# A Mamba/mLSTM/MoE block and a Hyena/RWKV block in one kernel: which engine makes the experts' low parts, and how the Hyena filters' last layer is multiplied

## The chip, the cores and the metric

The kernel runs on one core of a Trainium2 chip. The metric is the device time of one execution in microseconds (us): the median over the runs. Engines are named as in the profile: PE (TensorE matmul), PEld (its weight load), DVE (VectorE), ACT (ScalarE), POOL (GpSimd), SP (SyncE, which here only issues DMAs).

## The reference

One sequence of 1,024 tokens with 1,024 features passes two blocks. The first block mixes by an SSD and an mLSTM half and then by a mixture of 32 experts, two of them for each token. The second block mixes by Hyena (long convolutions, whose filters come from a small network) and RWKV halves, and ends with a feed-forward layer. Two pieces matter here:

```python
def hier_moe(h, wg, bg, we, be, w_gate, w_up, w_down):
    ...
    hg = lax.ragged_dot(xs, w_gate.astype(xs.dtype), sizes)
    hu = lax.ragged_dot(xs, w_up.astype(xs.dtype), sizes)
    ys = lax.ragged_dot(jax.nn.silu(hg) * hu, w_down.astype(xs.dtype), sizes)
    ...

def hyena_filters(L, fw1, fb1, fw2, fb2, fw3, fb3, fw4, sin_freq):
    ...
    h = jnp.sin(sf[0] * (feats @ fw1.astype(f32) + fb1.astype(f32)))
    h = jnp.sin(sf[1] * (h @ fw2.astype(f32) + fb2.astype(f32)))
    h = jnp.sin(sf[2] * (h @ fw3.astype(f32) + fb3.astype(f32)))
    h = (h @ fw4.astype(f32)).reshape(L, HY_ORDER, 2, HY_WIDTH)
    ...
    window = jnp.exp(-t * deltas[None, :])
    return h * window[:, None, None, :]
```

`fw4` has 64 rows and 2 x 2 x 512 columns. Everything is float32, and the filters depend on no token.

## The kernel before, in words

**How a float32 product is made.** `split` (lines 108 to 116) cuts a float32 tile into a high part, a copy of type F32R made by ScalarE (line 112), and a low part, the tile less the high part, an F32R tile made by a subtraction on VectorE or on an engine that the caller names (line 113). A product then is three F32R matmuls: high by high, high by low and low by high (`mm3`, line 125, and the experts' own loops at lines 989 and 1010). Matmuls on plain F32 operands are used in few places; the filter network is one.

**Experts (lines 954 to 1014).** Each of the 32 experts handles up to 128 gathered tokens (a loop behind them takes what is over). GpSimd clears the tile `X` (line 960) and gathers the tokens (961); PE transposes them, and `split` makes XTh and XTl. `wload` (972) fetches a weight matrix in pieces of 512 KB from a ring of raw buffers (`eraw`, and for the first experts also `ahead`), and splits it into `ewh` and `ewl`, four buffers each. There are four such pieces (q = 0 to 3) for each of the three matrices, 12 for each expert. The low part of piece q = 1 is made on GpSimd and the other three on VectorE: in all 96 on GpSimd and 288 on VectorE, which also makes the low parts of the tokens and of the hidden activations (XTl, Hl) and the gating (995, 996). ScalarE writes the expert's output `Y` (1012), and GpSimd adds it to memory by a scattered DMA (1013). SP issues the loads of the raw buffers.

**Filters (lines 1152 to 1250).** From expert 8 on, `moe` advances a generator once for each expert, so that the filters of the second block are computed between the experts' steps. It loads the small network and the DFT matrix, runs three sine layers of 64 outputs (matmul 1183, VectorE 1184 to 1191, Sin on ScalarE 1193), reorders the last one into `h3` by two VectorE copies (1198), and then, for each of two orders and two halves of the channels, loads 64 x 2 x 256 of `fw4` (1204) and for eight blocks of 128 positions makes two F32 products of 256 columns with 64 rows in the contraction (1215), multiplies each by the window on VectorE (`hfb`, 1217), and forms their sum and their difference on GpSimd (`hsum` 1220, `hd` 1223). These are split (`hsh` on ScalarE, `hsl` on VectorE, 115 and 116) and go through a DFT of F32R matmuls; GpSimd combines its outputs (`HR`, `HS`, line 1252).

**What sets the order.** The program is written as generators that advance in turn, and the Tile framework then lists each engine's instructions by a simulated timeline of the whole program. An edit can therefore move instructions on any engine, also far behind the place that it touches. One such place is the end of the RWKV recurrence: `rwkv_norm` (1957 to 1995) reads the recurrence's output `ytok`, adds its two directions, normalises (`ya`, ScalarE, line 1983) and transposes it (1987), while the last chunk of the recurrence still runs (`cup` on PE, line 1771; its copy `cUV` on ScalarE, 1775; `cyp` on PE, 1804; `cY`, 1811; `ytok`, 1813), and the gated projection of the Hyena output (`rwkv_out`, 2014: `yr<-hz_d`, `mwr`, then matmuls `mps<-yrh,mwh` through line 125) waits to start on the same queues.

Of the kernel before, what the change touches and what calls it, by code (L numbers as in the profile page):

```python
# [20 lines left out]
F32 = mybir.dt.float32  # L21
F32R = mybir.dt.float32r
# [3 lines left out]
ALU = mybir.AluOpType  # L26
# [4 lines left out]
P = 128  # L31
# [10 lines left out]
def f32(ap):  # L42
    return ap.bitcast(F32)
# [6 lines left out]
class Kern:  # L50
# [904 lines left out]
    def expert(self, ep, psm, pst, pg, gi, gate, wg, wu, wd, next_raw):  # L955
# [198 lines left out]
    def hyena_filters(self, psm, p, w):  # L1154
# [3 lines left out]
        self.hs_d = self.dp.tile([2, 2, P, 4, 512], F32, name="hs_d")  # L1158
        feats = w.tile([33, L], F32, name="feats", tag="hA", bufs=1)
        nc.sync.dma_start(feats, T["c_feats"])  # L1160
        fw = [p.tile([n, 64], F32, name=f"fw{i}") for i, n in enumerate((33, 64, 64))]
        for i in range(3):
            nc.sync.dma_start(fw[i], I[f"hy_filt_w{i + 1}_2"][0])
        fb = p.tile([64, 3], F32, name="fb")
        sf = p.tile([64, 3], F32, name="sf")
        for i in range(3):
            nc.sync.dma_start(fb[:, i:i + 1], I[f"hy_filt_b{i + 1}_2"][0].rearrange("(p o) -> p o", o=1))
        nc.sync.dma_start(sf, I["hy_sin_freq_2"][0].rearrange("l p -> p l"), allow_slow_non_contiguous=True)
# [6 lines left out]
        h = feats  # L1175
        MAGIC = 12582912.0
        for i in range(3):
            a = w.tile([64, L], F32, name="fa", tag="HR", bufs=1)
            n = w.tile([64, L], F32, name="fn", tag="HS", bufs=1)
            for half in range(2):  # L1180
                sl = slice(half * 512, half * 512 + 512)
                ps = psm.tile([64, 512], F32, name="fps", tag="s")
                nc.tensor.matmul(ps, fw[i], h[:, sl], start=True, stop=True)
                nc.vector.tensor_scalar(a[:, sl], ps, fb[:, i:i + 1], sf[:, i:i + 1], op0=ALU.add, op1=ALU.mult)
# [7 lines left out]
            h = w.tile([64, L], F32, name="fh", tag="hA", bufs=1)  # L1192
            nc.scalar.activation(h, a, AF.Sin)
            yield
        h3 = p.tile([64, 8, P], F32, name="h3")

        for mb in range(2):
            nc.vector.tensor_copy(h3[:, mb * 4:mb * 4 + 4],
                                  h[:, mb * 512:mb * 512 + 512].rearrange("p (m r) -> p r m", r=4))
        for o in range(2):  # L1200
            for half in range(2):
                ch = slice(half * 256, half * 256 + 256)
                fw4 = w.tile([64, 2, 256], F32, name="fw4")
                nc.sync.dma_start(fw4, w4[:, o, :, ch])
                sk = w.tile([1, 256], F32, name="hsk", bufs=1)
                nc.sync.dma_start(sk, I["hy_skip_2"][:, o, ch])
                sp = [p.tile([P, 8, 256], F32R, name=f"hs{x}") for x in "hl"]
                hd = p.tile([P, 8, 256], F32, name="hd")
                for b in range(8):
                    win = w.tile([P, 256], F32, name="win")  # L1210
                    nc.scalar.activation(win, delt[:, ch], AF.Exp, scale=tcol[:, b:b + 1])
                    hf = []
                    for d in range(2):
                        ps = psm.tile([P, 256], F32, name="fps2", tag="s")
                        nc.tensor.matmul(ps, h3[:, b], fw4[:, d], start=True, stop=True)
                        t = w.tile([P, 256], F32, name=f"hfb{d}")
                        nc.vector.tensor_tensor(t, ps, win, op=ALU.mult)
                        hf.append(t)
                    s_ = w.tile([P, 256], F32, name="hsum", bufs=1)
                    nc.gpsimd.tensor_tensor(s_, hf[0], hf[1], op=ALU.add)  # L1220
                    if b == 0:
                        nc.vector.tensor_tensor(s_[0:1], s_[0:1], sk, op=ALU.add)
                    nc.gpsimd.tensor_tensor(hd[:, b], hf[0], hf[1], op=ALU.subtract)
                    self.split(sp[0][:, b], sp[1][:, b], s_, 1.0 / 1024.0)
                    if b % 2:
                        yield
                for kb in range(2):
                    HR = w.tile([P, 4, 256], F32, name="HR", bufs=1)
                    ab, ch_ = self.dft(psm, w, Fh, Fl, sp, kb, "C")
                    _, d = self.dft(psm, w, Fh, Fl, sp, kb, "S", (1,))  # L1230
                    self.bf(HR[:, 0], ab[:, 0], ab[:, 1], ALU.add)
                    self.bf(HR[:, 1], ab[:, 0], ab[:, 1], ALU.subtract)
                    self.bf(HR[:, 2], ch_[:, 0], d[:, 0], ALU.add)
                    self.bf(HR[:, 3], ch_[:, 0], d[:, 0], ALU.subtract)
                    nc.sync.dma_start(self.hr_d[o, kb][:, :, ch], HR)
                    yield
                sp = [p.tile([P, 8, 256], F32R, name=f"hs{x}") for x in "hl"]
                for b in range(8):
                    self.split(sp[0][:, b], sp[1][:, b], hd[:, b], 1.0 / 1024.0)
                for kb in range(2):  # L1240
                    HS = w.tile([P, 4, 256], F32, name="HS", bufs=1)
                    ef, gd = self.dft(psm, w, Fh, Fl, sp, kb, "S")
                    _, h_ = self.dft(psm, w, Fh, Fl, sp, kb, "C", (1,))
                    self.bf(HS[:, 0], ef[:, 0], ef[:, 1], ALU.add)
                    self.bf(HS[:, 1], ef[:, 1], ef[:, 0], ALU.subtract)
                    self.bf(HS[:, 2], h_[:, 0], gd[:, 0], ALU.subtract)
                    self.bf(HS[:, 3], h_[:, 0], gd[:, 0], ALU.add)
                    nc.sync.dma_start(self.hs_d[o, kb][:, :, ch], HS)
                    yield
# [1052 lines left out]
```

## Time and profile before

| | |
|---|---|
| median of three runs | 3980.1 us (3979.16 to 3992.83) |
| the profiled execution's own time | 3969.92 us |
| its span in the trace | 3967.6 us |
| mean granted clock of PE | 0.937 |
| busy share PE, PEld, DVE, ACT, POOL | 89%, 72%, 72%, 38%, 39% |
| low parts `ewl<-eraw` on VectorE | 243, mean 1658 ns |
| low parts `ewl<-eraw` on GpSimd | 81, mean 2658 ns |

The span runs from the first to the last recorded instruction; the profiled execution took 2.3 us more than that, and 10.2 us less than the median. Busy shares are averages over stages with different limits, so the rows below are read stage by stage: the experts without filter work (1214 to 1352 us after the span's start), the experts with filter work (1352 to 1905), and the end of the RWKV recurrence (around 3017 to 3046).

### The profile page before, as it was taken

Reading aid. Unit: us, or ns where it says so; the run is one execution under the profiler, and the core shown is the slowest. Engines: PE = TensorE matmul, PEld = TensorE weight load, DVE = VectorE, ACT = ScalarE, POOL = GpSimd, SP = SyncE. Lnnn points to the kernel's source line nnn. Section 1 sums busy time; section 2 is a strip of 40 time slices with the busy share of each in tenths; the row PEclk is TensorE's granted clock in tenths of the full one; section 3 lists DMA queues with packets and bytes.
Section 4 is the critical chain, followed back from the end, with each engine's and each line's share of the span. In section 5 each row is a group of like instructions: output and inputs, shape, how many; then the busy total and the mean of one; then the engine's idle time right before and its main releaser. Section 6 shows DMA issues by size and latency. Waiting matters only on the chain. (4 is left out here: it accounts for less than half of the span.)

```text
span 3967.6 us, 52346 instructions
## 1 busy us (share of the span) xinstructions
PE 3544.1 (89%) x19799; PEld 2845.8 (72%) x19799; DVE 2861.4 (72%) x3992; ACT 1503.4 (38%) x2166; POOL 1540.5 (39%) x882
## 2 busy tenths in 40 slices
PE   6999897988978889999879999999776999999897
PEld 6888776666766667777656767887564777888775
DVE  7767858776457889998755887411995577777798
ACT  4332333433226766666633333222123213222331
POOL 4444434553015568777601222000771212223353
PEclk8999997899979999999989999999887999999998
DMA  4222224444568778888854777666556722222521
GB/s 102 96 85 107 97 74 148 137 151 145 182 208 285 233 247 287 294 268 274 280 153 132 213 207 194 185 192 220 161 170 195 258 103 69 85 75 95 177 94 69
DMA packets 540591, 669.34 MB, mean 169 GB/s; under 512 B 151819, under 2 KB 352015, under 8 KB 539824
## 3 DMA queue, kind: packets, MB, share of 16 engines
q1 hardware_dynamic: 429136, 535.38, 42.3%
q10 hardware_dynamic: 101984, 113.79, 8.4%
q0 software_dynamic: 9216, 16.81, 1.9%
q8 instruction: 157, 2.57, 0.3%
q14 instruction: 98, 0.80, 0.1%
HBM read 500.72 MB, written 181.83 MB: 172 GB/s over the span
## 5 line engine op out<-in xcount | busy, mean ns | idle before, releaser
L113 DVE TENSOR_TENSOR ewl<-eraw,ewh 128x1024 fp32r<-128x1024 f32 x243 | 398.8, 1658 | 40.6 <-ACT ewh L112 40.3
L112 ACT CAST ewh<-eraw 128x1024 fp32r<-128x1024 f32 x324 | 334.5, 1049 | 114.1 <-PE pgu L989 51.5
L125 PE MATMUL g<-x2h,wl 128*128 128x512 f32 x688 | 279.2, 406 | 0.0
L125 PE MATMUL g<-x2h,wh 128*128 128x512 f32 x688 | 278.9, 406 | 0.1
L125 PE MATMUL g<-x2l,wh 128*128 128x512 f32 x688 | 277.7, 404 | 0.0
L125 PE MATMUL g<-h,sw 128*128 128x512 f32 (+1 forms) x752 | 243.9, 401 | 20.5 <-ACT sw L112 9.6
L113 POOL TENSOR_TENSOR ewl<-eraw,ewh 128x1024 fp32r<-128x1024 f32 x81 | 215.3, 2658 | 111.1 <-ACT ewh L112 103.0
L163 POOL TENSOR_TENSOR sraw<-sraw 128x1024 f32<-128x1024 f32 x24 | 74.0, 3083 | 431.8 <-DVE sw L113 419.9
L125 PE MATMUL g<-xl,sw 128*128 128x512 f32 x616 | 241.5, 392 | 0.0
L989 PE MATMUL pgu<-ewl,XTh 128*128 128x512 f32 x512 | 210.5, 411 | 28.6 <-POOL ewl L113 18.0
L112 ACT CAST sw<-sraw 128x1024 fp32r<-128x1024 f32 x144 | 148.8, 1048 | 207.0 <-PE g L125 156.2
L125 PE MATMUL g<-z 128*128 128x512 f32 x820 | 201.7, 395 | 22.7 <-DVE z L113 19.7
L125 PE MATMUL g<-sw,h 128*128 128x256 f32 x960 | 184.6, 294 | 22.9 <-DVE sw L113 17.8
L989 PE MATMUL pgu<-ewh,XTh 128*128 128x512 f32 x512 | 204.2, 401 | 0.7 <-ACT XTh L112 0.7
L989 PE MATMUL pgu<-ewh,XTl 128*128 128x512 f32 x512 | 202.8, 396 | 0.0
L125 PEld LDWEIGHTS g<-z 128*128 128x128 f32 x820 | 155.1, 190 | 60.0 <-DVE z L113 23.0
L125 PEld LDWEIGHTS g<-h,sw 128*128 128x128 f32 (+1 forms) x752 | 143.2, 191 | 57.1 <-ACT sw L112 10.5
L113 DVE TENSOR_TENSOR wl<-raw,wh 128x1024 fp32r<-128x1024 f32 x43 | 52.6, 1223 | 173.1 <-ACT wh L112 167.7
L125 PEld LDWEIGHTS g<-sw,h 128*128 128x128 f32 x960 | 158.0, 202 | 23.9 <-DVE sw L113 18.6
L113 POOL TENSOR_TENSOR sw<-sraw,sw 128x1024 fp32r<-128x1024 f32 x39 | 102.5, 2628 | 179.9 <-ACT sw L112 179.9
L499 DVE SCALAR_TENSOR_TENSOR u<-sC,cw,u 128x1023 f32<-128x1023 f32 (+2 forms) x84 | 164.6, 1975 | 1.7 <-ACT u L497 1.4
L193 DVE TENSOR_TENSOR sC<-sU,g 128x512 f32<-128x512 f32 x140 | 95.2, 682 | 89.1 <-PE g L125 86.5
(684 smaller groups left out, 10113.7 us busy)
## 6 DMA issues: line engine op xcount, KB each, us to landing
eraw<-in_exp_w_down SPq DMA_DIRECT2D x112, 512.0 KB, 5.7
eraw<-in_exp_w_up SPq DMA_DIRECT2D x108, 512.0 KB, 4.7
eraw<-in_exp_w_gate SPq DMA_DIRECT2D x104, 512.0 KB, 5.6
sraw<-in_w_in SPq DMA_DIRECT2D x12, 2048.0 KB, 7.8
raw<-in_w_in ACTq DMA_DIRECT2D x43, 512.0 KB, 4.5
SC<-SC SPq DMA_DIRECT2D x32, 512.0 KB, 3.6
cSA<-X SPq DMA_DIRECT2D x32, 512.0 KB, 4.6
cSC<-SC SPq DMA_DIRECT2D x32, 512.0 KB, 7.6
```

Source lines behind the costliest of these rows:

```text
L112: nc.scalar.copy(h, raw)
L113: (eng or nc.vector).tensor_tensor(l, raw, f32(h), op=ALU.subtract)
L125: nc.tensor.matmul(ps, a, b, start=i == 0, stop=i == n - 1)
L163: Q(A11, A11, A21, op=ALU.subtract)
L193: V(c, x, ps, op=ALU.add)
L499: nc.vector.scalar_tensor_tensor(u[:, j:], x[:, :L - j], cw[:, ct, 3 - j:4 - j], u[:, j:], op0=ALU.mult, op1=ALU.add)
L989: nc.tensor.matmul(ps, a[:, q * 2 + k], b[:, k], start=q == 0 and k == 0 and i == 0, stop=q == 3 and k == 1 and i == 2)
```

## The change

The diff, cut to its core:

```diff
         def wload(w, q, down=False):
             shape = [P, D] if down else [P, 2, 512]
-            eng = nc.gpsimd if q == 1 else nc.vector
             raw = next_raw(self.piece(w, q, down))
...
-            self.split(h, l, raw, eng=eng)
+            self.split(h, l, raw)
             return h, l
...
-        fw = [p.tile([n, 64], F32, name=f"fw{i}") for i, n in enumerate((33, 64, 64))]
+        fw = [p.tile([n, m], F32, name=f"fw{i}") for i, (n, m) in enumerate(((33, 64), (64, 64), (64, P)))]
+        fb = p.tile([P, 3], F32, name="fb")
+        sf = p.tile([P, 3], F32, name="sf")
...
+            for o in range(0, fw[i].shape[1], 64):
+                nc.sync.dma_start(fw[i][:, o:o + 64], I[f"hy_filt_w{i + 1}_2"][0])
+        for o in (0, 64):
...
-        h3 = p.tile([64, 8, P], F32, name="h3")
+        h3 = p.tile([P, 8, P], F32R, name="h3")
         for mb in range(2):
-            nc.vector.tensor_copy(h3[:, mb * 4:mb * 4 + 4],
-                                  h[:, mb * 512:mb * 512 + 512].rearrange("p (m r) -> p r m", r=4))
+            x = h[:, mb * 512:mb * 512 + 512].rearrange("p (m r) -> p r m", r=4)
+            b = h3[:, mb * 4:mb * 4 + 4]
+            nc.scalar.copy(b, x)
+            nc.vector.tensor_tensor(b[64:], x[64:], f32(b)[64:], op=ALU.subtract)
...
-                fw4 = w.tile([64, 2, 256], F32, name="fw4")
-                nc.sync.dma_start(fw4, w4[:, o, :, ch])
+                fw4 = w.tile([P, 2, 256], F32, name="fw4")
+                for q in (0, 64):
+                    nc.sync.dma_start(fw4[q:q + 64], w4[:, o, :, ch])
+                fw4s = [w.tile([P, 2, 256], F32R, name=f"fw4{x}", bufs=1) for x in "hl"]
+                self.split(*fw4s, fw4)
...
-                    hf = []
-                    for d in range(2):
-                        ps = psm.tile([P, 256], F32, name="fps2", tag="s")
-                        nc.tensor.matmul(ps, h3[:, b], fw4[:, d], start=True, stop=True)
-                        t = w.tile([P, 256], F32, name=f"hfb{d}")
-                        nc.vector.tensor_tensor(t, ps, win, op=ALU.mult)
-                        hf.append(t)
+                    ps = psm.tile([P, 2, 256], F32, name="fps2", tag="s")
+                    for i in range(2):
+                        nc.tensor.matmul(ps, h3[:, b], fw4s[i], start=i == 0, stop=i == 1)
+                    hf = w.tile([P, 2, 256], F32, name="hfb")
+                    nc.vector.tensor_tensor(hf, ps, win[:, None, :].to_broadcast([P, 2, 256]), op=ALU.mult)
...
-                    nc.gpsimd.tensor_tensor(s_, hf[0], hf[1], op=ALU.add)
+                    nc.gpsimd.tensor_tensor(s_, hf[:, 0], hf[:, 1], op=ALU.add)
```

The first part gives all 384 low parts of the expert weights to VectorE. The second part computes the third sine layer twice, on partitions 0 to 63 and again on 64 to 127 (its weights, biases and frequencies are loaded twice). Then `h3` holds the high part of the layer's output in its first 64 partitions and the low part in the other 64, `fw4` stands in both halves and is split into a high and a low tile, and one contraction over 128 partitions with each of the two gives the whole product: for each block two F32R matmuls of 512 columns instead of two F32 ones of 256, and one multiplication of 128 x 512 instead of two of 128 x 256. The sums and differences on GpSimd stay.

The order of the instructions moves with it. On VectorE, among the first experts (`ewl_...` comes from raw buffers with running numbers), the low parts that GpSimd had fall into place between the others:

```order
 L113 TENSOR_TENSOR ewl<-eraw_9613,ewh 128x1024
+L113 TENSOR_TENSOR ewl<-eraw_9625,ewh 128x1024
 L113 TENSOR_TENSOR ewl<-eraw_9637,ewh 128x1024
 L113 TENSOR_TENSOR ewl<-eraw_9649,ewh 128x1024
 L113 TENSOR_TENSOR XTl<-pt,XTh 128x512
 L113 TENSOR_TENSOR ewl<-eraw_9675,ewh 128x1024
+L113 TENSOR_TENSOR ewl<-eraw_9687,ewh 128x1024
```

One low part in four is new in VectorE's queue, and the tokens' and the hidden activations' low parts stand behind it.

On ScalarE at the end of the RWKV recurrence, before (`cY`, `ytok`, `cUV` belong to the last chunks, `ya` and `yb` to the normalisation):

```order
L1811 COPY cY<-cyp 128x512
L1813 DMA ytok<-cY 64x512 x2
L1983 ACTIVATE ya<-ya,gnm,gr_y 128x64 x8
L1775 COPY cUV<-cup 64x512 x2
L1989 ACTIVATE yb<-pt,gnb,gnw 128x128 x4
L1983 ACTIVATE ya<-ya,gnm,gr_y 128x64 x8
L1811 COPY cY<-cyp 128x512
L1813 DMA ytok<-cY 64x512 x2
```

and the same place of the changed kernel, whose lines count 8 higher:

```order
L1819 COPY cY<-cyp 128x512
L1821 DMA ytok<-cY 64x512 x2
L1783 COPY cUV<-cup 64x512 x2
L1991 ACTIVATE ya<-ya,gnm,gr_y 128x64 x8
L1819 COPY cY<-cyp 128x512
L1991 ACTIVATE ya<-ya,gnm,gr_y 128x64 x8
L1821 DMA ytok<-cY 64x512 x2
L1997 ACTIVATE yb<-pt,gnb,gnw 128x128 x8
```

The last chunk's two copies `cUV` move from behind the eight `ya` to ahead of them.

On SP at the same place, before and then changed (`yr<-hz_d` is the first load of the gated projection):

```order
L1752 DMA cUV<-vt 64x512
L1965 DMA ya<-ytok 128x512
L1969 DMA obv<-bv 128x4x128
L1994 DMA yr<-yb 128x4x128
L1971 DMA og<-g 128x4x128
L1965 DMA ya<-ytok 128x512
L1967 DMA yb<-ytok 128x512
L2024 DMA yr<-hz_d 128x1024
```

```order
L1760 DMA cUV<-vt 64x512
L1973 DMA ya<-ytok 128x512
L2032 DMA yr<-hz_d 128x1024
L2009 DMA mwr<-in_w_hy_out 128x4x128
L2016 DMA mtg<-tg_d 128x512 x2
L2009 DMA mwr<-in_w_hy_out 128x4x128
L1973 DMA ya<-ytok 128x512
```

The projection's first loads move ahead of the next `ya` load and of the write of `yr` from `yb`, behind which they stood.

## Rows read from the trace of the kernel before

**Rows 1.** Windows: us, then PE, PEld, DVE, ACT, POOL busy (instructions), granted clock, DMA share, GB/s.

```profile
1214.00:1352.00 138.00, 119.44 (x512) 93.91 (x511) 111.69 (x93) 93.93 (x109) 74.40 (x35) 0.94 0.77 253
1352.00:1905.00 553.00, 512.54 (x2456) 397.51 (x2454) 507.17 (x510) 374.86 (x493) 406.87 (x251) 0.98 0.83 275
```

**Rows 2.** Waits, 1352 to 1905 us: engine, what waited <- for what: us, times, longest.

```profile
PE pgu L989 <- POOL ewl L113: 17.8, 11, 5.6
```

**Rows 3.** Timeline of DVE and POOL from 1433.5 us: start, duration.

```profile
1433.96 2.39 POOL L113 TENSOR_TENSOR ewl<-eraw,ewh 128x1024 fp32r<-128x1024 f32 x1 [1.80 <-issue]
...
1434.76 2.66 DVE L113 TENSOR_TENSOR ewl<-eraw,ewh 128x1024 fp32r<-128x1024 f32 x1
```

**Rows 4.** Instructions of three tiles, whole span: duration in ns min/median/max.

```profile
L113 DVE TENSOR_TENSOR ewl<-eraw,ewh x243: 1202/1214/5149, 1192.0 to 1966.4; 128x1024 fp32r<-128x1024 f32 x122
...
L116 DVE SCALAR_TENSOR_TENSOR hsl<-hd,hsh x32: 407/412/3283, 1515.4 to 1883.0; 128x256 fp32r<-128x256 f32 x32
...
L1220 POOL TENSOR_TENSOR hsum<-hfb,hfb x32: 718/1584/2238, 1429.2 to 1845.4; 128x256 f32<-128x256 f32 x32
```

**Rows 5.** Groups by line, 1214 to 1352 us: busy us, mean ns | idle before, releaser.

```profile
L113 DVE TENSOR_TENSOR ewl<-ahead,ewh 128x1024 fp32r<-128x1024 f32 x34 | 57.5, 1707 | 16.9 <-ACT ewh L112 16.8
...
L113 POOL TENSOR_TENSOR ewl<-ahead,ewh 128x1024 fp32r<-128x1024 f32 x11 | 30.4, 2762 | 26.5 <-ACT ewh L112 26.4
L113 DVE TENSOR_TENSOR ewl<-eraw,ewh 128x1024 fp32r<-128x1024 f32 x20 | 30.1, 1517 | 12.5 <-ACT ewh L112 12.5
...
L113 POOL TENSOR_TENSOR ewl<-eraw,ewh 128x1024 fp32r<-128x1024 f32 x6 | 16.0, 2666 | 20.1 <-ACT ewh L112 20.0
```

**Rows 6.** The same view, 1352 to 1905 us.

```profile
L113 DVE TENSOR_TENSOR ewl<-eraw,ewh 128x1024 fp32r<-128x1024 f32 x189 | 314.8, 1681 | 20.3 <-ACT ewh L112 20.0
...
L113 POOL TENSOR_TENSOR ewl<-eraw,ewh 128x1024 fp32r<-128x1024 f32 x64 | 169.6, 2650 | 68.6 <-ACT ewh L112 60.5 <-issue 7.8
...
L1215 PE MATMUL fps<-fw,h 64*128 64x256 f32 x128 | 41.6, 419 | 1.1 <-DVE hfb L1217 0.8 <-DVE h L1198 0.3
...
L116 DVE SCALAR_TENSOR_TENSOR hsl<-hsum,hsh 128x256 fp32r<-128x256 f32 x32 | 32.3, 1010 | 3.1 <-ACT hsh L115 2.8
...
L113 DVE TENSOR_TENSOR XTl<-pt,XTh 128x512 fp32r<-128x512 f32 x42 | 28.5, 678 | 1.8 <-ACT XTh L112 1.7
...
L116 DVE SCALAR_TENSOR_TENSOR hsl<-hd,hsh 128x256 fp32r<-128x256 f32 x32 | 26.6, 896 | 0.0
L1217 DVE TENSOR_TENSOR hfb<-fps,win 128x256 f32<-128x256 f32 x64 | 25.7, 412 | 7.9 <-PE fps L1215 6.2 <-POOL hsum L1220 1.7
```

**Rows 7.** Timeline of PE at 1430.9 and at 1612 us.

```profile
1430.88 0.70 PE L1215 MATMUL fps<-fw,h 64*128 64x256 f32 x2
1431.50 0.50 PE L1010 MATMUL g<-ewh,Hh 128*128 128x512 f32 x1
...
1612.06 0.39 PE L1010 MATMUL g<-ewl,Hh 128*128 128x512 f32 x1
1612.29 0.39 PE L1010 MATMUL g<-ewh,Hl 128*128 128x512 f32 x1
```

**Rows 8.** Waits, 1214 to 1352 us.

```profile
PE g L1010 <- DVE Hl L113: 11.0, 5, 2.2
```

**Rows 9.** Timeline at the end of the RWKV recurrence, 3017 to 3047 us.

```profile
3017.04 1.97 PE L1771 MATMUL cup<-cX,cSA 64*64 64x64 f32 x32 [0.32 <-ACT cX L1763]
...
3025.67 2.76 ACT L1983 ACTIVATE ya<-ya,gnm,gr_y 128x64 f32<-128x64 f32 x8 [8.21 <-DVE gnm L1981]
3028.34 1.17 ACT L1775 COPY cUV<-cup 64x512 f32<-64x512 f32 x2
3028.95 2.57 PE L1804 MATMUL cyp<-cUV,cSC 128*64 128x64 f32 x32
...
3038.57 0.42 SPq L2024 DMA_DIRECT2D yr<-hz_d  x1
...
3046.32 1.22 PE L125 MATMUL mps<-yrh,mwh 128*128 128x512 f32 x2 [11.95 <-ACT mwh L112]
```

More of the change, by code (lines that the diff above doesn't have):

```diff
@@ L1160, in hyena_filters @@
         nc.sync.dma_start(feats, T["c_feats"])
-        fw = [p.tile([n, 64], F32, name=f"fw{i}") for i, n in enumerate((33, 64, 64))]
+        fw = [p.tile([n, m], F32, name=f"fw{i}") for i, (n, m) in enumerate(((33, 64), (64, 64), (64, P)))]
+        fb = p.tile([P, 3], F32, name="fb")
+        sf = p.tile([P, 3], F32, name="sf")
         for i in range(3):
[L1163 to L1168, printed above, removed]
+            for o in range(0, fw[i].shape[1], 64):
+                nc.sync.dma_start(fw[i][:, o:o + 64], I[f"hy_filt_w{i + 1}_2"][0])
+        for o in (0, 64):
+            for i in range(3):
+                nc.sync.dma_start(fb[o:o + 64, i:i + 1], I[f"hy_filt_b{i + 1}_2"][0].rearrange("(p o) -> p o", o=1))
+            nc.sync.dma_start(sf[o:o + 64], I["hy_sin_freq_2"][0].rearrange("l p -> p l"), allow_slow_non_contiguous=True)
         w4 = I["hy_filt_w4_2"][0].rearrange("k (o d c) -> k o d c", o=2, d=2)
@@ L1177, in hyena_filters @@
         for i in range(3):
-            a = w.tile([64, L], F32, name="fa", tag="HR", bufs=1)
-            n = w.tile([64, L], F32, name="fn", tag="HS", bufs=1)
+            m = fw[i].shape[1]
+            a = w.tile([m, L], F32, name="fa", tag="HR", bufs=1)
+            n = w.tile([m, L], F32, name="fn", tag="HS", bufs=1)
             for half in range(2):
                 sl = slice(half * 512, half * 512 + 512)
-                ps = psm.tile([64, 512], F32, name="fps", tag="s")
+                ps = psm.tile([m, 512], F32, name="fps", tag="s")
                 nc.tensor.matmul(ps, fw[i], h[:, sl], start=True, stop=True)
-                nc.vector.tensor_scalar(a[:, sl], ps, fb[:, i:i + 1], sf[:, i:i + 1], op0=ALU.add, op1=ALU.mult)
+                nc.vector.tensor_scalar(a[:, sl], ps, fb[:m, i:i + 1], sf[:m, i:i + 1], op0=ALU.add, op1=ALU.mult)
             nc.vector.tensor_scalar(n, a, 1.0 / (2.0 * math.pi), MAGIC, op0=ALU.mult, op1=ALU.add)
@@ L1191, in hyena_filters @@
             nc.vector.tensor_scalar(a, a, 3.1415925, -3.1415925, op0=ALU.min, op1=ALU.max)
-            h = w.tile([64, L], F32, name="fh", tag="hA", bufs=1)
+            h = w.tile([m, L], F32, name="fh", tag="hA", bufs=1)
             nc.scalar.activation(h, a, AF.Sin)
             yield
-        h3 = p.tile([64, 8, P], F32, name="h3")
+        h3 = p.tile([P, 8, P], F32R, name="h3")
         for mb in range(2):
-            nc.vector.tensor_copy(h3[:, mb * 4:mb * 4 + 4],
-                                  h[:, mb * 512:mb * 512 + 512].rearrange("p (m r) -> p r m", r=4))
+            x = h[:, mb * 512:mb * 512 + 512].rearrange("p (m r) -> p r m", r=4)
+            b = h3[:, mb * 4:mb * 4 + 4]
+            nc.scalar.copy(b, x)
+            nc.vector.tensor_tensor(b[64:], x[64:], f32(b)[64:], op=ALU.subtract)
         for o in range(2):
@@ L1211, in hyena_filters @@
                     nc.scalar.activation(win, delt[:, ch], AF.Exp, scale=tcol[:, b:b + 1])
-                    hf = []
-                    for d in range(2):
-                        ps = psm.tile([P, 256], F32, name="fps2", tag="s")
-                        nc.tensor.matmul(ps, h3[:, b], fw4[:, d], start=True, stop=True)
-                        t = w.tile([P, 256], F32, name=f"hfb{d}")
-                        nc.vector.tensor_tensor(t, ps, win, op=ALU.mult)
-                        hf.append(t)
+                    ps = psm.tile([P, 2, 256], F32, name="fps2", tag="s")
[3 more added lines that the diff above has]
+                    nc.vector.tensor_tensor(hf, ps, win[:, None, :].to_broadcast([P, 2, 256]), op=ALU.mult)
                     s_ = w.tile([P, 256], F32, name="hsum", bufs=1)
-                    nc.gpsimd.tensor_tensor(s_, hf[0], hf[1], op=ALU.add)
+                    nc.gpsimd.tensor_tensor(s_, hf[:, 0], hf[:, 1], op=ALU.add)
                     if b == 0:
                         nc.vector.tensor_tensor(s_[0:1], s_[0:1], sk, op=ALU.add)
-                    nc.gpsimd.tensor_tensor(hd[:, b], hf[0], hf[1], op=ALU.subtract)
+                    nc.gpsimd.tensor_tensor(hd[:, b], hf[:, 0], hf[:, 1], op=ALU.subtract)
                     self.split(sp[0][:, b], sp[1][:, b], s_, 1.0 / 1024.0)
```

## The prediction

> **What bounds the kernel now.** The change touches the expert loop, so I read that stretch first, by windows. Without filter work the experts run from 1214 to 1352 us, with filter work from 1352 to 1905 [rows 1]. In the second window PE is busy 512.5 of 553 us and VectorE 507.2, both over nine tenths, ScalarE 374.9 and GpSimd 406.9. Neither PE nor VectorE alone sets the pace: PE loses 40.5 us, of which 17.8 are matmuls that wait for a low part that GpSimd is still making [rows 2], and VectorE in turn sits 20.0 us until ScalarE has copied a high part [rows 6]. So work taken from one of the two can pay only as far as the other follows.
>
> Next I asked whether VectorE's 507 us are work. At 1434 us GpSimd's subtraction runs from 1433.96 for 2.39 us, to 1436.35. VectorE's subtraction of two SBUF tiles starts at 1434.76 and takes 2.66 us, until 1437.42 [rows 3]: it ends about 1.1 us behind GpSimd's. The same subtraction has a median of 1.214 us and a minimum of 1.202 [rows 4], but means of 1.707, 1.517 and 1.681 in the two windows [rows 5, 6]. I read this as an exclusive resource: while GpSimd works on two SBUF tiles, a VectorE instruction with two SBUF inputs stands still and is recorded as busy. Window products, which read PSUM and one SBUF tile, keep a mean of 0.412 in the same stretch, where two-tile instructions of the same 128 x 256 have means of 1.010 and 0.896 and a median of 0.412 [rows 4, 6]. [...]
>
> **Price of a low part on GpSimd.** Without filter work, 34 + 20 subtractions take VectorE 57.5 + 30.1 = 87.6 us [rows 5]; undisturbed they would take 54 x 1.214 = 65.6 [rows 4]. The 22.0 us over are due to 11 + 6 = 17 GpSimd low parts: 1.30 us each. On VectorE itself each costs 1.214. So moving a low part hardly adds to VectorE: it pays nearly this price already.
>
> With filter work the excess is 314.8 - 189 x 1.214 = 85.4 us on the weights' low parts and 32.3 + 26.6 - 64 x 0.412 = 32.5 on the filters' own [rows 4, 6], 118 in all. At 1.30 us the 64 GpSimd low parts explain 83; the remaining 35 belong to the other GpSimd tensor work, 128 filter additions by the loops of the program. Had the 64 all of it, each would cost 1.84.
>
> **The change, part by part, with filter work.** VectorE: -83 of standing, +64 x 1.214 = +77.7; 64 window products at 0.412 become 32 of twice the size, which I price like the tokens' low part (128 x 512, one input from PSUM, 0.678): 21.7 for 25.7, -4.0; four low parts of `fw4` at the same 0.678, +2.7; the subtractions that replace the copies into `h3` are two instructions for two, taken as zero. Sum -7, or -42 if all 118 us went. PE: two F32 products stand as one pair from 1430.88 to 1431.50, 0.62 us for each window block and direction; there are 128 records, thus 64 products at 0.62 = 39.7 us. In their place come 64 F32R matmuls of 512 columns, 12.29 - 12.06 = 0.23 us from start to start [rows 6, 7]: 14.7. PE saves 25.0. The wider third sine layer keeps its count of matmuls and costs nothing. ScalarE gains four copies of `fw4` and two into `h3`, some 5 us at its 374.9 of 553: covered. The doubled loads of `fw4` are 0.5 MB more, about 2 us at 275 GB/s; the DMA share of 0.83 leaves room for them, so zero [rows 1]. They and five small loads more go through SP's queue ahead of raw buffers. A wide load issues in 0.42 us there [rows 9], so nine take some 4 us, and as the single columns of biases may be slower, I keep 8 us as the worst, if no raw buffer were loaded early enough to cover them.
>
> What the stage makes of it has two ends. If VectorE paces it at its present share, 507.2/553 = 0.917, 500 us of work take 545: -8. If PE paces it, 487.5 us of work with the present 40.5 idle take 528 (-25), and without the 17.8 us of waits for GpSimd 510 (-43). I take **-25**: PE's saving is certain, a wait on GpSimd's 2.65 us instruction becomes at worst one on VectorE's 1.21, and VectorE then needs a share of 500/528 = 0.947, little above what it holds.
>
> **Without filter work** VectorE goes from 111.7 to 111.7 - 22.0 + 17 x 1.214 = 110.3, -1.4. But PE waits 11.0 us for the low part of the hidden activations [rows 8], which stands behind the weights' low parts on VectorE and is late by whatever holds one of them 2.7 us long. Between 1.4 and 11 I take **-3**, nearer the busy sum, because one more subtraction per matrix now stands ahead of it. The other 96 - 81 = 15 moved low parts lie before and behind these windows; at 1.30 against 1.21 they give nothing.
>
> **A side effect far behind.** Before, the eight `ya` activations on ScalarE start only at 3025.67, after a wait of 8.21 us for VectorE, and the copies `cUV` stand behind them until 3028.34, though `cup` was done at 3019.0. PE's `cyp` follows at 3028.95, `yr<-hz_d` on SP at 3038.57, and the first projection matmul at 3046.32, after 11.95 us of PE idle [rows 9]. In the new order `cUV` goes ahead of `ya`, so that it can run some 9 us earlier, and `yr<-hz_d` no longer stands behind the later loads. What is late next is the normalisation itself, whose VectorE work doesn't change. The path gives 3028.34 - 3019.0 = 9.3 us, at most the 11.95 us of PE idle plus the 8.21 of ScalarE; at worst a reordered queue costs 5. I take **-9**.
>
> **Sum.** -25 - 3 - 9 = -37 against the profiled execution's 3969.9, so 3933; that execution is 10.2 us under the median of the runs, against which I give the forecast: 3980.1 - 37 = **3943**. A measurement of this kernel can tell about 0.5% (20 us) from no change, so faster means below 3960 and slower above 4000.
>
> **Rivals.**
> 1. *VectorE becomes the bound, and the time rises.* GpSimd's filter additions stay and find VectorE inside a two-tile subtraction, or hold it up, more often than now. Each holds at least 0.72 us [rows 4]; 128 make 92 us, of which VectorE stands 35 today. At its share of 0.917 the stage is longer than before once VectorE loses more than 35 + 7 = 42 us to them. At 80 us VectorE has 545, the stage takes 594 (+41), and with -3 and -9 the kernel 4009. For it: VectorE is already at 0.917. Against it: products out of PSUM pass freely [rows 6], and fewer GpSimd instructions leave fewer to collide with. The Trainium skill speaks for this rival (Perfetto Trace Analysis, Optimizing Scalar/DVE Operations): a full VectorE should hand work to other engines, even GpSimd, and the change does the opposite; the same paragraph doubts the gain because of the shared port, and 1.30 against 1.214 here bears that doubt out. Chance 0.06, with any gain refused because the long subtractions had another cause.
> 2. *VectorE paces, without new collisions.* The stage gives -8, the first window -1, and the side effect between nothing and -9: 3980 - 9 to -18, about 3966. PE's saving lies then under VectorE. For it: the two shares differ by one hundredth. Chance 0.21.
> 3. *PE paces, and the waits on GpSimd go too.* -43 - 11 - 9 = -63: 3917, and down to 3903 if VectorE's excess also vanishes and the projection's start moves by more. For it: 17.8 us of PE's idle time name GpSimd. Against it: VectorE would need 500/510 = 0.98. Chance 0.15.
> 4. *The side effect doesn't come*, because the order follows a model of time and the chip's queues wait elsewhere: -28, 3952. This and the forecast share a sign; together they have 0.58.
>
> **How the numbers follow.** Faster: 0.58 + 0.15 = 0.73; within: 0.21; slower: 0.06. The range reaches from the low end of rival 3, 3903, to rival 2 with no side effect and half of the loads' worst, 3980 - 9 + 4 = 3975, and leaves out rival 1 and the tails.
>
> **What would show it.** Right: the 384 low parts on VectorE have a mean near 1.25 to 1.35 us, GpSimd has none; the window products are 32 at about 0.68; a pair of filter matmuls takes 0.46 us; the stretch with filter work lasts about 528 us, PE's waits name VectorE or ScalarE; `cUV` follows `cup` at once and the first projection matmul comes about 9 us earlier in its stage. Wrong: a mean above 1.45 us with GpSimd's additions beside it (rival 1), a filter stretch of 545 us with VectorE's share kept (rival 2), or a gain that lies in stages named nowhere above.

## The result and the profile after

The changed kernel takes 3912.9 us (median of four runs, 3903.1 to 3922.1) against 3979.6 of before on the same chips: ratio 0.984, 95% interval 0.9815 to 0.9864, about 64 us faster. The forecast was 3943 in a range from 3903 to 3975. So sign and range held, but the gain is nearly double the forecast's 37 us, and the time lies where rival 3 was put (3917).

In the trace the span goes from 3967.6 to 3908.5 us. From the seventh expert's output `Y` (line 1012; 1011 after the change) to the last one's, the experts with filter work and those behind them took 621.0 us before, from 1351.9 to 1972.9. The windows of that stretch, before and then after (columns as in [rows 1]); the second line of after is the filter stretch alone, the third the experts without filters:

```profile
1351.90:1972.90 621.00, 577.08 (x2743) 448.23 (x2741) 561.10 (x556) 422.54 (x547) 447.09 (x268) 0.98 0.84 277
```

```profile
1334.80:1908.00 573.20, 541.21 (x2680) 441.61 (x2680) 534.91 (x600) 428.03 (x554) 266.50 (x195) 0.98 0.90 299
...
1335.00:1844.00 509.00, 481.65 (x2417) 394.79 (x2418) 482.52 (x549) 382.10 (x504) 259.31 (x191) 0.98 0.90 300
...
1206.50:1335.00 128.50, 113.19 (x509) 89.25 (x507) 107.62 (x111) 92.95 (x108) 24.53 (x18) 0.98 0.83 277
```

By the times of the experts' `Y`: the first comes 7.6 us earlier than before, the next six take 9.5 us less, the filter stretch 44.4 less (553.6 to 509.2), the last four experts 3.5 less. That is about 65 at the end of the experts. Behind them 5.8 are lost again: 3.9 are gained around the projection and some 9.6 lost in stretches whose work didn't change. In the twelve profiles of this study, all with the same work there, the stretch from the experts to the recurrence's last state product lasts 1034 to 1048 us and the one behind the projection 809 to 820, so this loss is no effect of the change that can be told from chance. Part of the first output's 7.6 us may be chance too: it comes at 1206.2 us here and between 1207.5 and 1212.2 in the eight runs below that also keep the weights' low parts off GpSimd and have no idle reader, against 1213.7 before and 1215.8 with the filters alone.

The groups by line of the filter stretch, 1335 to 1844 us, answer to [rows 6]:

```profile
L113 DVE TENSOR_TENSOR ewl<-eraw,ewh 128x1024 fp32r<-128x1024 f32 x254 | 326.2, 1309 | 12.8 <-ACT ewh L112 11.9
...
L988 PE MATMUL pgu<-ewl,XTh 128*128 128x512 f32 x336 | 137.5, 409 | 8.6 <-DVE ewl L113 8.5
...
L988 PE MATMUL pgu<-ewh,XTh 128*128 128x512 f32 x337 | 134.0, 402 | 8.4 <-ACT ewh L112 8.4
...
L1231 POOL TENSOR_TENSOR hd<-hfb 128x256 f32<-128x256 f32 x32 | 51.9, 1626 | 25.5 <-DVE hfb L1226 25.3
...
L1226 DVE TENSOR_TENSOR hfb<-fps,win 128x512 f32<-128x512 f32 x32 | 21.8, 680 | 10.6 <-POOL hsum L1228 10.6
...
L116 DVE SCALAR_TENSOR_TENSOR hsl<-hsum,hsh 128x256 fp32r<-128x256 f32 x32 | 17.4, 544 | 0.0
...
L116 DVE SCALAR_TENSOR_TENSOR hsl<-hd,hsh 128x256 fp32r<-128x256 f32 x32 | 15.5, 551 | 0.0
...
L1224 PE MATMUL fps<-fw4h,h 128*128 128x512 f32 x32 | 13.6, 424 | 4.6 <-DVE hfb L1226 4.5
```

The reader is to see three things. The low parts' mean fell from 1681 to 1309 ns and the filters' own from 1010 and 896 to 544 and 551: VectorE now stands 326.2 - 254 x 1.214 = 17.8 and 17.4 + 15.5 - 64 x 0.412 = 6.5, together 24 us instead of 118. The window product costs 680 ns, the price forecast. And no matmul waits for GpSimd directly any more: the 17.8 us of [rows 2] are gone, and the experts' products wait for low parts from VectorE (8.5 us) and for high parts from ScalarE (8.4). One wait has grown, VectorE's window product for GpSimd's `hsum`, from 1.7 us [rows 6] to 10.6, with PE's next filter product behind it (4.5).

### The profile page after: what moved, and what is told of

It reads as the page before. It is cut to its first block, busy times and chain, and to the rows that moved or that the text cites. A ratio compares the mean times of both kernels' runs of the same rounds, so it can differ in the third digit from the quotient of the medians.

```text
span 3908.5 us, 52188 instructions
## 1 busy us (share of the span) xinstructions
PE 3508.2 (90%) x19735; PEld 2838.5 (73%) x19735; DVE 2836.2 (73%) x4060; ACT 1508.4 (39%) x2174; POOL 1295.9 (33%) x786
## 5 line engine op out<-in xcount | busy, mean ns | idle before, releaser
L113 DVE TENSOR_TENSOR ewl<-eraw,ewh 128x1024 fp32r<-128x1024 f32 x324 | 409.3, 1291 | 23.8 <-ACT ewh L112 18.8
L113 DVE TENSOR_TENSOR sw<-sraw,sw 128x1024 fp32r<-128x1024 f32 x105 | 135.3, 1303 | 34.2 <-ACT sw L112 33.3
L125 PEld LDWEIGHTS g<-x2h,wl 128*128 128x128 f32 x688 | 131.7, 191 | 37.9 <-issue 10.3
```

Of the source, the lines that this page charges most:

```text
L113: (eng or nc.vector).tensor_tensor(l, raw, f32(h), op=ALU.subtract)
L125: nc.tensor.matmul(ps, a, b, start=i == 0, stop=i == n - 1)
```

## Experiments

Throughout, **the stage** means the stretch from the seventh expert's output to the last one's, found again in each trace; shares are busy time by its length. A ratio is to the kernel before on the same chip. Differences in us between two kernels are of medians, and as the runs are from several chips, on which the kernel before had medians of 3972.7 to 3979.6, they are good to a few us. In the expectations, *port* stands for the exclusive resource of the prediction, and *standing* for the time that a VectorE instruction is recorded as busy while it waits for that resource.

| kernel | ratio, 95% | stage us | PE share | VectorE share |
|---|---|---|---|---|
| before | 1 | 621.0 | 0.929 | 0.904 |
| changed | 0.984 (0.9815 to 0.9864) | 573.2 | 0.944 | 0.933 |
| low parts only | 0.9851 (0.983 to 0.9872) | 586.0 | 0.970 | 0.921 |
| filters only | 1.0045 (1.0028 to 1.0062) | 634.1 | 0.887 | 0.905 |
| idle reader | 1.0261 (1.0237 to 1.0286) | 688.7 | 0.863 | 0.959 |
| idle writer | 0.9901 (0.9877 to 0.9926) | 588.0 | 0.934 | 0.907 |
| sums in weights | 0.9769 (0.9744 to 0.9793) | 546.8 | 0.970 | 0.954 |
| more PE | 0.9811 (0.9787 to 0.9835) | 562.4 | 0.981 | 0.953 |
| more VectorE | 0.9823 (0.9799 to 0.9848) | 565.4 | 0.962 | 0.972 |
| two buffers at the end | 0.9844 (0.9819 to 0.9869) | 573.1 | 0.945 | 0.933 |
| deeper buffers | 0.9812 (0.9782 to 0.9841) | 568.0 | 0.951 | 0.949 |
| sums in weights, plain F32 | 0.9838 (0.9806 to 0.9869) | 577.3 | 0.963 | 0.908 |

**1. Each part alone.** From before, with low parts only:

```diff
-            eng = nc.gpsimd if q == 1 else nc.vector
...
-            self.split(h, l, raw, eng=eng)
+            self.split(h, l, raw)
```

> Only the first part: all low parts of the expert weights on VectorE, the filters as before. Theory A (port, and both engines pace the stage): VectorE loses the standing of 96 GpSimd low parts, gains 96 x 1.214 us; without filter work the experts take about 10 us less for seven of them, as in the changed kernel; with filter work PE still has its 512 us, at the changed kernel's fill of 0.946 that is 541, 12 less than before; together with the first expert and the last ones about 30 to 35 us faster than before, ratio about 0.992. Theory B (PE's matmul time made the gain): the stage keeps its 553 us, the kernel is within 10 us of before.

and the changed kernel with the opposite edit, so that only the filters differ from before:

> Only the second part: stacked filters, a quarter of the low parts still on GpSimd. Theory A: PE's 25 us are saved but VectorE, standing 1.3 to 1.5 us for each of 64 GpSimd low parts, still has about 506 us of the stretch with filter work and paces it; 0 to 10 us faster than before, ratio 0.998 to 1.000. Theory B: PE's saving comes out in full, about 25 us faster, ratio 0.994. If the two parts simply add, this one and the one with low parts alone give together the 64 to 67 us of the whole change.

Measured: low parts only 3915.4 us against 3972.7, 57 faster; filters only 3988.9, 16 *slower*. The first part alone is thus worth nearly the whole change, far more than the 30 to 35 expected, and the second alone costs time. They don't add: 1.49 - 0.45 = 1.04 per cent against 1.60. The stage's window with low parts only, and its waits of PE:

```profile
1333.30:1919.30 586.00, 568.28 (x2742) 446.28 (x2740) 539.53 (x631) 425.89 (x549) 255.58 (x195) 0.99 0.89 294
...
PE g L1009 <- DVE Hl L113: 8.1, 3, 4.2
PE pgu L988 <- DVE ewl L113: 2.7, 3, 1.7
```

VectorE's busy time fell from 561 to 540 us although it makes a third more low parts, and PE's idle time from 44 to 18: PE, 0.970 busy, is now clearly the fuller engine. The 35 us of the stage have two sources that no run takes apart: less standing on VectorE, and no more waits of PE for GpSimd's late low parts. Of the filters alone, the window, the groups and the waits, and behind them the low parts and the longest wait of PE in the same stretch of before:

```profile
1353.60:1987.70 634.10, 562.22 (x2681) 445.89 (x2680) 573.83 (x529) 428.93 (x557) 445.90 (x268) 0.97 0.83 273
...
L113 DVE TENSOR_TENSOR ewl<-eraw,ewh 128x1024 fp32r<-128x1024 f32 x219 | 366.0, 1689 | 28.7 <-ACT ewh L112 28.5
...
L1010 PE MATMUL g<-ewl,Hh 128*128 128x512 f32 x200 | 84.3, 422 | 25.5 <-DVE ewl L113 17.1 <-POOL ewl L113 8.4
...
L116 DVE SCALAR_TENSOR_TENSOR hsl<-hsum,hsh 128x256 fp32r<-128x256 f32 x32 | 39.4, 1231 | 0.7 <-ACT hsh L115 0.5
...
PE pgu L989 <- POOL ewl L113: 15.2, 15, 2.7
PE pgu L989 <- DVE ewl L113: 11.3, 11, 3.5
```

```profile
L113 DVE TENSOR_TENSOR ewl<-eraw,ewh 128x1024 fp32r<-128x1024 f32 x218 | 359.3, 1664 | 26.8 <-ACT ewh L112 26.5
...
PE pgu L989 <- POOL ewl L113: 18.0, 12, 5.6
```

PE is busy 15 us less there, but VectorE has 13 more, 574 us, at the share it had before (0.905 beside 0.904). PE's saving became waiting time: its waits for low parts are 52.0 us (17.1 + 8.4 + 15.2 + 11.3), against 30.3 before. This speaks for VectorE, with the low parts still on GpSimd, as what paces the kernel before; one pair of runs whose orders differ doesn't prove it. Eleven of the 13 us are standing: 366.0 - 219 x 1.214 = 100.1 on the weights' low parts and 39.4 + 24.5 (the other group of `hsl`) - 26.4 = 37.5 on the filters', 138 in all, against 359.3 - 218 x 1.214 = 94.6 and 32.5, 127 in all, in the same stretch of before. Why VectorE stands longer there isn't settled; the order moved too.

**2. Is it the port, or GpSimd's late results?** The changed kernel with idle work on GpSimd, pinned in time by reading the piece's high part; a reader and a writer:

```diff
             self.split(h, l, raw)
+            if q == 1:
+                for i in range(2):
+                    nc.gpsimd.tensor_tensor(self.dz, hv[:, i * 512:i * 512 + 512], self.dz, op=ALU.subtract)
```

```diff
+            if q == 1:
+                nc.gpsimd.tensor_copy(self.dz[:, :8], hv[:, :8])
+                for _ in range(4):
+                    nc.gpsimd.memset(self.dz, 0.0)
```

(`hv` is the high part, `dz` a scrap tile of 128 x 512.)

> The changed kernel, and for each piece that GpSimd used to split, two GpSimd subtractions of 128 x 512 on SBUF tiles whose result nobody uses. Theory A (port): VectorE stands 1.3 to 1.5 us for each of 96 such pairs although nobody waits for GpSimd's results; VectorE's low parts go back from a mean of 1.29 us to about 1.6, the stretch with filter work goes up by 60 to 100 us, the kernel by 70 to 120. Rival L (what cost was the late result, PE waiting for a low part that takes GpSimd 2.65 us): no matmul waits for these, the time stays within 10 us of the changed kernel's 3913.

> The changed kernel, and for each piece that GpSimd used to split, one GpSimd copy of 128 x 8 and four memsets of 128 x 512, about the same GpSimd time as the two subtractions, which write SBUF and read nothing. Theory A (a reader holds what VectorE's second input needs): no standing, within 10 us of the changed kernel's 3913. Rival (any GpSimd work on SBUF holds VectorE up, or GpSimd's queue delays the gathers): as slow as the idle reader, 70 us and more above.

Measured: 4074.8 and 3935.1 us, 162 and 22 above the changed kernel. Groups by line of the stage, reader (with its window ahead and a wait of ScalarE behind) and then writer, and last the changed kernel's low parts in the same stage:

```profile
1382.80:2071.50 688.70, 594.67 (x2680) 453.15 (x2680) 660.45 (x599) 429.70 (x555) 534.80 (x341) 0.95 0.78 249
...
L113 DVE TENSOR_TENSOR ewl<-eraw,ewh 128x1024 fp32r<-128x1024 f32 x292 | 469.0, 1639 | 9.5 <-ACT ewh L112 9.4
...
L981 POOL TENSOR_TENSOR dz<-ewh,dz 128x512 f32<-128x512 f32 x146 | 281.8, 1930 | 63.3 <-ACT ewh L112 58.5
...
L992 PE MATMUL pgu<-ewl,XTh 128*128 128x512 f32 x384 | 169.2, 441 | 47.9 <-DVE ewl L113 46.6
...
ACT ewh L112 <- POOL dz L981: 35.2, 17, 5.6
```

```profile
L113 DVE TENSOR_TENSOR ewl<-eraw,ewh 128x1024 fp32r<-128x1024 f32 x292 | 366.5, 1286 | 18.6 <-ACT ewh L112 18.2
L982 POOL MEMSET dz<- 128x512 f32 x292 | 163.6, 560 | 13.8
...
L1233 DVE TENSOR_TENSOR hfb<-fps,win 128x512 f32<-128x512 f32 x32 | 21.8, 683 | 22.1 <-POOL hsum L1235 22.0
```

```profile
L113 DVE TENSOR_TENSOR ewl<-eraw,ewh 128x1024 fp32r<-128x1024 f32 x292 | 370.9, 1299 | 17.2 <-ACT ewh L112 16.3
```

With the reader nobody needs the result of the idle work, yet VectorE's low parts are back at 1639 ns, its share is 0.959 and PE waits for it. The reader has one side effect: it holds the buffer of the high part that it reads, and ScalarE waits 35.2 us for such buffers. VectorE, at 0.959, waits for late high parts for only 9.5 us, so that isn't what lengthens the stage. In the stage the standing is 469.0 - 292 x 1.214 = 114 instead of 370.9 - 354.5 = 16 (the changed kernel's 292 low parts take 370.9 there): 98 us for 73 pairs, 1.3 us each, on these instructions alone. The writer holds GpSimd for 164 + 57 us in the stage and leaves the low parts at 1286. So what stands VectorE up is GpSimd *reading* SBUF; the Trainium skill (SBUF — State Buffer, Who interferes with whom) makes the same distinction, and these two runs agree. The reader cost more than expected (162 where 70 to 120 stood), and the writer's 22 us were expected to stay within 10. Its likely cause is GpSimd's longer queue, in which the filters' sums come late (22.0 us of VectorE's waits, 10.6 without it); no run separates that from the order.

**3. What paces the changed kernel?** More work on either engine:

```diff
+                    for _ in range(3):
+                        nc.tensor.matmul(ps, h3[:, b], fw4s[0], start=True, stop=True)
                     for i in range(2):
                         nc.tensor.matmul(ps, h3[:, b], fw4s[i], start=i == 0, stop=i == 1)
```

> The changed kernel with 96 more F32R matmuls of 512 columns in the filters (three ahead of each pair, overwritten by it): about 96 x 0.227 = 21.8 us of PE work, near the 25 us that the change saved. PE paces: expert stage 20 us or more longer. VectorE paces: expert stage within 6 us of the changed kernel's 573. What the run with low parts alone suggests (its PE is 0.97 busy, and with PE's 27 us less the stage fell by only 13): about half, 8 to 14 us.

```diff
                     nc.vector.tensor_tensor(hf, ps, win[:, None, :].to_broadcast([P, 2, 256]), op=ALU.mult)
+                    nc.vector.tensor_tensor(hf, ps, win[:, None, :].to_broadcast([P, 2, 256]), op=ALU.mult)
```

> The changed kernel with each window product (128 x 512 out of PSUM, 0.680 us) made twice: 32 x 0.680 = 21.8 us of VectorE work that doesn't touch what GpSimd shares. VectorE paces: at its share of 0.933 the expert stage is 23 us longer. PE paces: within 6 us. Both in turn: about half.

Measured: 3900.8 and 3905.7 us. Neither is slower than the changed kernel; their stages are 11 and 8 us *shorter* (562.4 and 565.4), with 22 us more work by the expectations' sums, of which 10 and 15 us show as busy time. Every expectation missed. Their windows:

```profile
1338.20:1900.60 562.40, 551.45 (x2776) 457.50 (x2776) 536.17 (x600) 427.86 (x554) 259.05 (x195) 0.99 0.91 305
```

```profile
1339.30:1904.70 565.40, 543.97 (x2677) 437.07 (x2678) 549.56 (x629) 429.83 (x554) 261.52 (x193) 0.99 0.90 303
```

PE reaches 0.981 in the one, VectorE 0.972 in the other. So in the changed kernel, at 0.944 and 0.933, neither was full. I take it that its order of instructions leaves some time unused, since each edit gave the framework another order (the end of the filters moves from 1843 us to 1853 and 1908). One suspect for the unused time was the new wait on `hsum`, so it got deeper buffers:

```diff
-                    hf = w.tile([P, 2, 256], F32, name="hfb")
+                    hf = w.tile([P, 2, 256], F32, name="hfb", bufs=3)
...
-                    s_ = w.tile([P, 256], F32, name="hsum", bufs=1)
+                    s_ = w.tile([P, 256], F32, name="hsum", bufs=2)
```

> The changed kernel with three buffers instead of two for the window products and two instead of one for their sum. Theory C (with PE at 0.944 and VectorE at 0.933 neither is full in the changed kernel; its order lets them run into the chain product, window, GpSimd's sum and difference, buffer free again, on which VectorE loses 10.6 us and PE 4.5 + 5.7): those waits go, the expert stage falls from 573 to about 560, the kernel 8 to 15 us under the changed kernel. Rival (VectorE's work sets the stage in every order): within 4 us of 573, ratio as the changed kernel's.

Measured: 3903.9 us, 9 less by medians, with ratios whose intervals overlap. The stage fell to 568.0, 5 and not 13. The wait itself went, as the waits of the stage show (VectorE's 10.6 and PE's 5.7 for `hsh` before it):

```profile
DVE hfb L1226 <- POOL hsum L1228: 0.7, 1, 0.7
...
PE pgu L988 <- ACT ewh L112: 11.6, 6, 6.9
...
PE dps L125 <- ACT hsh L115: 1.5, 3, 0.7
```

but PE's waits for ScalarE's high parts went from 8.4 + 1.8 to 11.6 + 6.1. The chain through GpSimd may be a part of the loss; the remainder stays open, since no run here held the order still.

**4. Taking GpSimd's filter sums away, and what the stacking is worth then.** The two directions' weights are added and subtracted before the split, so that the products are already sum and difference:

```diff
+                nc.vector.tensor_tensor(fwx[:, 0], fw4[:, 0], fw4[:, 1], op=ALU.add)
+                nc.vector.tensor_tensor(fwx[:, 1], fw4[:, 0], fw4[:, 1], op=ALU.subtract)
...
-                    nc.gpsimd.tensor_tensor(s_, hf[:, 0], hf[:, 1], op=ALU.add)
+                    s_ = hf[:, b, 0]
...
-                    nc.gpsimd.tensor_tensor(hd[:, b], hf[:, 0], hf[:, 1], op=ALU.subtract)
```

> The changed kernel, but the sums and differences of the two directions are formed on the 64 x 512 weights before they are split (two VectorE subtractions or additions of 128 x 256 for each of four passes), so that the products come out as sum and difference and GpSimd's 64 filter additions of 128 x 256 are gone. Theory A (VectorE paces with PE, and a GpSimd reader costs VectorE time): the 24 us that VectorE still stands in the changed kernel about halve, the chain product, window, GpSimd, high part loses GpSimd's 1.4 to 1.6 us; the expert stage 5 to 15 us shorter than 573, the kernel 0 to 10 us under the changed kernel, since the end of the RWKV recurrence goes back to the order of before here (about 4 us). Rival (the remaining GpSimd work is free): expert stage within 4 us of 573.

Measured: 3887.4 us, ratio 0.9769, whose interval lies clear of the changed kernel's: faster than both kernels, 25 below the changed one where 0 to 10 stood. The stage is 546.8:

```profile
1337.00:1883.80 546.80, 530.25 (x2680) 438.57 (x2680) 521.88 (x604) 427.29 (x555) 193.67 (x131) 0.99 0.92 314
...
L113 DVE TENSOR_TENSOR ewl<-eraw,ewh 128x1024 fp32r<-128x1024 f32 x292 | 363.0, 1276 | 14.3 <-ACT ewh L112 13.3
...
L116 DVE SCALAR_TENSOR_TENSOR hsl<-hd,hsh 128x256 fp32r<-128x256 f32 x64 | 29.0, 487 | 0.0
```

VectorE's 535 us became 522, since its standing in the stage halved: 363.0 - 354.5 + 29.0 - 26.4 = 11 us, where the changed kernel has 16 + 6.5 = 23. The other half of the stage's 26 comes from both engines being fuller (0.970 and 0.954). The same without stacking, two F32 products of 64 rows:

> All low parts on VectorE and the sums and differences formed on the weights, so that GpSimd's 64 filter additions are gone, but the filters' last layer as two F32 products of 256 columns with 64 rows: the run with sums in the weights without the stacking. It shows what the stacking is worth where PE is nearly full (PE 0.970 busy there). Theory: PE paces then and its 25 us come out, expert stage 567 to 572 instead of 547, the kernel 18 to 25 us slower than that run's 3887. Rival (the stacking is worth nothing, as it seemed beside the run with low parts alone): within 6 us of 3887.

Measured: 3916.8 us, 29 slower than with the stacking, stage 577.3:

```profile
1332.40:1909.70 577.30, 556.21 (x2743) 446.63 (x2742) 523.99 (x605) 424.65 (x549) 175.22 (x131) 0.99 0.89 298
```

VectorE has 524 and 522 us in the two, PE 556 and 530. So the stacking's 25 us come out whole (30 in the stage) once GpSimd's sums are out of the way; beside them the stage fell by 13, and beside GpSimd's low parts it rose by 13. The order moved in each pair, and by section 3 it alone can make some 10 us, so only the 30 stands clear of it.

**5. The end of the recurrence.** In the changed kernel (timeline; to be held against [rows 9], from which it lies some 62 us earlier at the recurrence's last state product, 3009.8 and 2948.0):

```profile
2954.88 1.19 ACT L1783 COPY cUV<-cup 64x512 f32<-64x512 f32 x2 [1.18 <-PE cup L1779]
...
2960.66 2.76 ACT L1991 ACTIVATE ya<-ya,gnm,gr_y 128x64 f32<-128x64 f32 x8 [4.60 <-DVE gnm L1989]
...
2964.39 0.42 SPq L2032 DMA_DIRECT2D yr<-hz_d  x1
...
2974.14 1.22 PE L125 MATMUL mps<-yrh,mwh 128*128 128x512 f32 x2 [3.05 <-ACT mwh L112]
...
2981.99 1.04 ACT L112 CAST yrh<-yr 128x1024 fp32r<-128x1024 f32 x1 [6.51 <-DMA yr<-hz_d]
2983.09 1.22 PE L125 MATMUL mps<-yrh,mwh 128*128 128x512 f32 x2 [6.02 <-ACT yrh L112]
```

`cUV` follows `cup`, and the first projection matmul comes 26.2 us after that product instead of 36.5, as forecast. Then ScalarE waits 6.5 us for the second of four `yr` loads, which share one buffer, and the last projection matmul comes 143.0 after it instead of 146.9: 3.9 of 10 are kept. The one buffer isn't what took the rest, as the kernel before loads through one too, and the fourth `yr` is copied by ScalarE 47.6 us after the product instead of 57.3, 9.7 earlier. Windows of 40 us, from 20 and from 60 us after that product, before and then changed (columns as in [rows 1]):

```profile
3029.80:3069.80 40.00, 19.36 (x95) 11.49 (x94) 16.77 (x70) 19.34 (x47) 6.46 (x6) 0.54 0.64 197
3069.80:3109.80 40.00, 37.61 (x159) 30.03 (x159) 21.31 (x28) 10.13 (x14) 4.14 (x3) 0.98 0.91 305
```

```profile
2968.00:3008.00 40.00, 23.02 (x57) 13.92 (x57) 20.45 (x69) 15.99 (x37) 6.34 (x5) 0.58 0.66 205
3008.00:3048.00 40.00, 37.18 (x157) 29.67 (x156) 18.11 (x25) 10.17 (x16) 2.13 (x2) 0.96 0.88 303
```

In both kernels PE, busy for half of the first window, has a granted clock of 0.54 and 0.58 there, nearer 1.2 than 2.4 GHz, and 0.98 and 0.96 in the second, in which it is busy nearly throughout. So the earlier start falls into slow time: 60 us after the product 46 of the projection's 384 matmuls have started instead of 21, and at the later pace of 87 in 20 us those 25 are worth 5.7 us, not 10. With `bufs=2` for `yr`:

> The changed kernel with two buffers instead of one for the rows yr that the gated projection loads after the RWKV recurrence. Theory: the projection now starts 10 us earlier after the recurrence's last state product than before (26.2 instead of 36.5), but gave 6 of them back because four loads go one after another through one buffer (issues 16.4, 28.2, 36.3 and 43.4 us after that product); with two the loads overlap, the last projection matmul comes 3 to 6 us earlier than the changed kernel's 143.0 after that product. Rival (the clock of PE, at half in this stretch, sets it): no change there. In the whole time, 0 to 6 us.

Measured: the loads are issued in pairs, and the last projection matmul comes 140.6 us after the product, 2.4 earlier and less than the 3 to 6 expected. The loads do come sooner, and 99 of the 384 matmuls have started after 60 us, but then PE waits for VectorE:

```profile
PE mps L125 <- DVE mtg L2019: 9.9, 5, 4.7
```

The whole, 3915.7, can't be told from the changed kernel. Of all the kernels, those with before's order on ScalarE reach the last projection matmul after 142.1 to 147.1 us and those with the new order and one buffer after 143.0 to 144.6, so the reordering's 3.9 us can't be told from the spread of single profiles.

## Why the prediction was right in its range, and wrong in its terms

- **What bounds the kernel: half right.** The exclusive resource and its reading side are shown (idle reader, idle writer), but it isn't only for instructions with two SBUF inputs (see the last section). "Neither PE nor VectorE alone sets the pace" isn't borne out for the kernel before: PE's saving alone shortens nothing there, VectorE keeps its share to two thousandths, and taking work from VectorE alone shortens the stage by 35 us.
- **The price of a GpSimd low part: too low.** 1.30 us each left 35 us of standing for the filters' additions; 24 were left. By the same account the 64 cost (118 - 24)/64 = 1.47 us each in the filter stretch. VectorE's sum went from 507.2 to 482.5, -25 instead of -7: 11 us more by that price, and some 7 from the sine layers and the copies into `h3`, which were priced at nothing and took 27.4 us before and 20.4 after, as some of them had stood too. In the stretch without filters 1.30 was right (mean of the low parts now 1.22).
- **The filter stretch, -25: mis-sized and put down to the wrong part.** The step "PE's saving is certain, a wait on GpSimd's 2.65 us instruction becomes at worst one on VectorE's 1.21" failed in its first half. The stretch gave -44.4, the size of rival 3, but not by its sum of two gains: low parts alone took it to 514.3 us, -39, with all of PE's F32 work still there. With PE's saving alone the stage is 13 us longer; beside the low parts it is 13 shorter; the saving comes out whole only when GpSimd's sums go too. That the time still fell within the range is in part luck: the range took in rival 3's size, and the runs reached that size by another route.
- **Without filter work, -3: too small.** It gave -9.5, and up to -7.6 ahead of the first output, counted as nothing. The upper end named there, 11 us of PE waiting for the hidden activations' low part, was the better guide: that wait is 3.9 us now, in six experts where VectorE is busy 107.6 us of 128.5. There a low part that comes when it should was worth more than the busy time it saved.
- **The side effect, -9: mechanism right, size off.** The start moved by 10 us, as forecast. The step that failed is that 10 us at the start are 10 at the end: they fell where PE's granted clock averages 0.58, and the 4 that were left are within the spread.
- **Rival 1** (VectorE loses to the filter's additions) fell for the whole change, since the standing shrank. The run with the filters alone comes nearest to it: there VectorE stands 138 us instead of 127, though not on the filters' additions alone.
- **The sum** of -37 came to -64 in the ratio and -59 in the span. The medians' 10 us above the profiled execution, carried along in the forecast, did no harm.

## What to carry to other kernels

A busy engine isn't a working one: compare an instruction's mean with its minimum before counting it as load, and price work on GpSimd by what it takes from VectorE. Here a 128 x 1024 subtraction on GpSimd cost VectorE 1.3 to 1.5 us and would have cost 1.21 to do itself. And price a saving only on the engine that paces the stage: with the same 25 us of PE saved, the stage was 13 us longer, 13 shorter and 30 shorter, by what stood beside them.

## What the runs showed that I had not expected

- Instructions with one SBUF input can stand too. In the kernel before, two clamps of the sine layers (line 1191: one tile of SBUF in, one out) and a copy into `h3` took 2.90, 2.85 and 1.88 us, each with a GpSimd low part under way when it started, and each ended about 0.5 us behind that; the third clamp, beside nothing but a gather's DMA on GpSimd, took 0.68. The first of them, on GpSimd and VectorE:

```profile
1365.80 2.41 POOL L113 TENSOR_TENSOR ewl<-eraw,ewh 128x1024 fp32r<-128x1024 f32 x1 [2.69 <-ACT ewh L112]
1365.86 2.90 DVE L1191 TENSOR_SCALAR fa<-fa 64x1024 f32<-64x1024 f32 x1
```

- Two kernels with 22 us more work than the changed one, on PE or on VectorE, have stages 11 and 8 us shorter. With a list order made by a model of time, an edit's effect of this size can be the order's and not the work's; differences under 10 us in this stage shouldn't be read as prices.
- An idle GpSimd writer that leaves VectorE's instructions alone still costs 22 us, probably by the queue: 128 filter additions stand in order with it.
- GpSimd's own additions didn't become quicker when its load fell: `hsum` and `hd` have means of 1367 and 1626 ns after and 1303 and 1284 before, with a minimum of 718 before [rows 4]. They seem to wait for VectorE as VectorE waits for them: in the changed kernel the 24 `hsum` that start while VectorE is inside a two-tile instruction take 1555 ns on average and the other eight 804. The two groups before, 1352 to 1905 us:

```profile
L1220 POOL TENSOR_TENSOR hsum<-hfb,hfb 128x256 f32<-128x256 f32 x32 | 41.7, 1303 | 18.6 <-DVE hsl L116 11.1 <-DVE hfb L1217 6.8 <-ACT ewh L112 0.8
...
L1223 POOL TENSOR_TENSOR hd<-hfb,hfb 128x256 f32<-128x256 f32 x32 | 41.1, 1284 | 5.5 <-DVE hfb L1217 5.5
```
